# One Hymba-style layer: a two-part spread of 1 / rms, the mixer's first weights placed inside the FFN, and another order of the mixer's last norms

## The chip, the cores and the metric

The kernel runs on one core of one Trainium2 chip. The metric is the device time of one execution in microseconds. A core has a matrix engine (TensorE, PE in the profile; PEld is its loading of weights), a vector engine (VectorE, DVE), a scalar engine (ScalarE, ACT), GpSimd (POOL) and SyncE (SP), which here only issues transfers. Each engine takes its own instructions in the order in which the program lists them, and waits on semaphores where it needs the work of another.

## The reference, cut to what matters

1,048 tokens (16 meta tokens, 1,024 prompt tokens, 8 sample tokens) go through one decoder layer of width 1,024 in float32:

```
h = h + 0.5 * swiglu(rmsnorm(h, n1), w1g, w1u, w1d)      # first FFN, hidden width 2816
u = rmsnorm(h, nm) @ w_in                                # the mixer's input projection
...  HGRN2 scan of 4 heads (q, f, v, gate g); Mamba-2 scan of 8 heads (x, B, C after a short convolution, gate z, dt)
o_hg = o_hg * rsqrt(mean(o_hg^2) + eps) * hg_norm * silu(g)           # per head of 128
yz   = y * silu(z); yz = yz * rsqrt(mean(yz^2) + eps) * ssm_norm      # two groups of 256
h = h + concat(o_hg, yz) @ w_out
h = h + 0.5 * swiglu(rmsnorm(h, n2), w2g, w2u, w2d)      # second FFN
y = rmsnorm(h, norm_final)
```

The outputs are y and the new states of both scans and of the convolution.

## The kernel before, in words

Tokens lie along the free dimension of the tiles, features on the 128 partitions. The 1,048 tokens are four quarters of 262 (`Q`), two of which make a half. A float32 product with full accuracy is made of three products in the faster format float32r (`mm3`, lines 169 to 171): each operand is split into a rounded part `hi` and a rest `lo`, and hi·hi, hi·lo and lo·hi are summed in PSUM. A split is one cast on ScalarE (L163, L497, L376) and one subtraction on VectorE (L164, L501, L382).

**The first FFN** runs from 0 to about 699 us. Gate and up matrices and the down matrix are multiplied by a Strassen-like scheme of seven block products; the operands of half 0 are `ops[0]` (`o` in the code), those of half 1 `ops[1]` (`e`), and `cast`, `low` and `sum_` prepare block p of them. The work is a list of steps (class `Steps`): step i is a block of matrix products, 12 of them for a quarter and 4 input tiles, and `S.before(i, fn)` puts other work in front of step i. Inside `manual_schedule` the four engines PE, DVE, ACT and SP keep exactly this order of writing; instructions written after it are placed by the framework's planner, which may put them into gaps ahead.

The input tiles are normalised late: the FFN's first product uses x times the norm's weights, and 1 / rms of each token is multiplied into the results. `Input.rms` (before step 24) computes 1 / rms with tokens on partitions (`st[:, 1]`, ten columns for ten tiles of up to 128 tokens), then ScalarE scales a unit matrix by it, ten times (L1425): a diagonal matrix for every tile, side by side in one tile `diag` of 1,048 columns. `spread_r(q)` (before step 28 + q) multiplies a matrix of ones by a quarter of it in full float32 (L1430), which puts 1 / rms of each token on all partitions, and ScalarE copies that from PSUM (L1431) into the tile `spread`. The products `spread_r` have four PSUM buffers (`psm`) in common with other work, two of which the FFN's steps 26 to 31 hold.

The FFN's last 24 steps, before its end `e1`, are the seventh product of the down matrix: first half 0 for four pairs of output tiles, then, from `e0` = `e1` - 12, half 1 for the same. After each pair VectorE adds the result to h (L1118), ScalarE squares it (L255), VectorE adds the square (L256). From `e0` + 2 on, the mixer's norm of quarters 0 and 1 is made (L185 to L191), and from `e0` + 3 on, two jobs of `plain_x` before each step make the mixer's input x: for each of eight tiles of a quarter VectorE multiplies (L327), ScalarE casts (L328), VectorE subtracts (L330). 18 such jobs for quarters 0 and 1 stand before steps `e0` + 3 to `e0` + 11; those of quarters 2 and 3 stand at `e1`.

**The mixer** starts in `ssm_project`: `proj_first` multiplies the first chunk of 350 tokens with the weights of three units of 128 columns (units 0, 1, 2), then the second chunk, then the third. Each unit's weights are two raw tiles of 512 columns (`raw`, 8 buffers), split into two tiles `ws` (6 buffers) by L163 and L164. All this is written after the FFN, and the planner places it: it put the six splits ahead of and among the x jobs.

**The end of the mixer**: `Fill` hands out projections (`z1`, `g3` are the last) as filling between the scans. Then come the norm of the second Mamba group (`ssm_norm(K, 1, ...)`, a list of seven functions with `Rms.root`, `newton`, four `part`s) and that of HGRN head 3 (`hgrn_out(K, 3, ...)`). `root` sums squares by products of 32 columns (L209), ScalarE takes the root by Ln and Exp after loading a table (L211 to L217), VectorE refines it (L221 to L223), `part` spreads it again (L229). The first norm's functions all stand before the second norm's. Then `out_proj` multiplies with w_out.

Of the kernel before, what the change touches and what calls it, by code (L numbers as in the profile page):

```python
# [17 lines left out]
P = 128  # L18
# [49 lines left out]
class Core:  # L68
# [72 lines left out]

    def ws(self, dt=F32R):
        return self.wsp.tile([P, 1024], dt, tag="ws", name=self.uid("ws"))

    def weights(self, ap):

# [14 lines left out]
    def split(self, src, hi, lo):  # L161

        self.nc.scalar.copy(hi, src)  # L163
        self.nc.vector.tensor_sub(lo, src, hi.bitcast(F32))  # L164
# [150 lines left out]
def new_x(K):  # L315
    K.xhi, K.xlo = ([K.slot("u", T, F32R) for k in range(KT)] for i in range(2))
# [159 lines left out]
class Left:  # L476
# [732 lines left out]
def constants(K, a):  # L1209
    nc = K.nc  # L1210
    cst = K.const
    K.ident = cst.tile([P, P], F32, name="ident")
    make_identity(nc, K.ident)
    K.ones = {}
    for n in (1, D):
        K.ones[n] = cst.tile([P, P], F32, name=f"ones{n}")
        nc.vector.memset(K.ones[n], 1.0 / n)
    K.eps = cst.tile([P, 1], F32, name="eps")
# [88 lines left out]
class Input:  # L1307
# [111 lines left out]
    def rms(self):  # L1419

        K = self.K
        token_rstd(K, *(self.st[:, j] for j in range(3)))
        self.diag = K.slot("u", T)
        for i, (t0, n) in enumerate(self.tiles):
            K.nc.scalar.activation(self.diag[:, t0 : t0 + n], K.ident[:, :n], AF.Identity, scale=self.st[:, 1, i : i + 1])  # L1425

    def spread_r(self, q):
        K = self.K
        ps = K.psm()[:, :Q]
        K.nc.tensor.matmul(ps, K.ones[1], self.diag[:, q * Q : q * Q + Q], start=True, stop=True)  # L1430
        K.nc.scalar.copy(self.spread.quarter(q), ps)  # L1431


# [23 lines left out]
def ssm_project(K, a, o):  # L1457

    nc = K.nc
    wv = a["w_in"][0].rearrange("(k p) c -> p k c", p=P)  # L1460
    pc = K.pc


    rw = K.st0.tile([P, KT, 8])
    nc.sync.dma_start(rw, wv[:, :, C_DT : C_DT + 8])
    wd = K.sml.tile([P, KT, 16], F32R, tag="wdt", name="wdt", bufs=1)
    nc.scalar.copy(wd[:, :, 0:8], rw)
    nc.vector.tensor_sub(wd[:, :, 8:16], rw, wd[:, :, 0:8].bitcast(F32))
# [12 lines left out]
    nc.sync.dma_start(sc, a["state_conv"].rearrange("l b j c -> (l b j) c"))  # L1481
    ps = K.psm()
    for k in range(8):
        nc.tensor.transpose(ps[:, 24 * k : 24 * k + 24], sc[:, k * P : (k + 1) * P], K.ident[:24, :24])
    sb = K.st0.tile([P, 8, 8, 3])

    tails = K.st0.tile([P, 11, 8])
    nc.vector.tensor_copy(sb.rearrange("p k b j -> p (k b j)"), ps[:, :192])

    K.xs = []  # L1490

    def unit(k):
# [10 lines left out]
        return (*K.weights(wv[:, :, C_X + k * P : C_X + (k + 1) * P]), ev)  # L1503
# [721 lines left out]
def body(ctx, tc, a, o):  # L2225
# [10 lines left out]
    def before(S, i, *fns):  # L2236
        for fn in fns:
            S.before(i, (lambda fn=fn: fn[0](*fn[1:])))

    def first1(S, w, w2):  # L2240
# [73 lines left out]
        before(S, 27, (e.low, 5), (e.cast, 7))  # L2314
        before(S, 28, (e.low, 7))
        for q in range(4):
            before(S, 28 + q, (x.spread_r, q))
        before(S, 33, (e.cast, 4))
        before(S, 34, (e.low, 4))

    def after1(S, h, e3, e0, e1):
# [17 lines left out]
        for q in (1, 3):  # L2339
            S.before(e3 + q + 7, lambda q=q: nm.begin(q))  # L2340
            S.before(e3 + q + 9, lambda q=q: nm.finish(q))
        S.before(e0, lambda: new_x(K))
        S.before(e0 + 2, lambda: nm.end(0))
        S.before(e0 + 2, lambda: x_mix(0))
# [35 lines left out]
    with K.tc.manual_schedule(engines={mybir.EngineType.PE}):  # L2380
# [29 lines left out]
                kept.append(g)  # L2410
        fill.until("z1")
        fill(4)
        for fn in ssm_norm(K, 1, "s", lambda: None):
            fill(3)
            fn()
        fill.until("g3")
    for i in range(len(opa), 4):
        opa.append(split_spilled(i))
    for fn in hgrn_out(K, 3, pieces, us[3]["g"], "u", lambda: None):
        fn()  # L2420
    kept.append(us[3]["g"])
    kept += [y[:, NM:] for y in K.y[2:]]
    K.tokens(TO)
# [144 lines left out]
```

## Time and profile before

| | us |
|---|---|
| median of 3 runs | 1923.13 (1920.56 to 1923.39) |
| the profiled execution's own time | 1922.67 |
| its span, first to last instruction | 1920.9 |
| PE busy | 1905.5 (99%) |
| DVE busy | 1526.5 (79%) |
| ACT busy | 858.0 (45%) |

The granted clock of TensorE is 0.998 of full speed. The ends of products are modelled in such a profile, so the distance from one product's start to the next one's is read, not its length: in the FFN a float32r product of 262 columns starts 0.12 us after the one before it. In a row of the timeline stand the start, the length, the engine, the line, the operation, what it writes and reads, its shape and count, and in brackets the engine's idle time before it with what ended it.

### The profile page before, as it was taken

What the parts mean: (1) busy time and instruction counts of PE and PEld (TensorE: products, weight loads), DVE (VectorE), ACT (ScalarE), POOL (GpSimd) and SP (SyncE); (2) the same over time, 40 slices, a digit from 0 to 9 for tenths busy, and PEclk for the clock granted to TensorE, in tenths of its full rate; (3) what the DMA queues carried; (4) which work ended last, traced back from release to release, by engine and by line L of the source; (5) the groups of instructions that cost most, each with busy time, mean ns of one, the idle gap of its engine ahead of it and who ended that gap; (6) DMA issues with size and microseconds to landing.
All of it is one profiled execution on the core that took longest, in us unless ns stands there. A gap on an engine that the chain in (4) does not pass through costs nothing.

```text
span 1920.9 us, 41195 instructions
## 1 busy us (share of the span) xinstructions
PE 1905.5 (99%) x16692; PEld 1875.2 (98%) x16692; DVE 1526.5 (79%) x2866; ACT 858.0 (45%) x1635; POOL 30.1 (2%) x88
## 2 busy tenths in 40 slices
PE   9999999999999999999999999999999999999998
PEld 9999999999999999999999999999999999999998
DVE  7888888889788877566585557999888888978974
ACT  6533333334534644466564545743333332453353
POOL 3000000000000000000000000000000000000000
PEclk9999999999999999999999999999999999999999
DMA  7143333335967541221463254133333333596852
GB/s 249 50 128 95 95 107 112 92 98 175 305 215 243 165 152 52 66 89 38 116 186 85 83 173 144 58 114 107 99 93 101 101 112 93 173 269 210 281 175 84
DMA packets 324209, 258.46 MB, mean 135 GB/s; under 512 B 18923, under 2 KB 298731, under 8 KB 324011
## 3 DMA queue, kind: packets, MB, share of 16 engines
q1 hardware_dynamic: 323779, 255.79, 43.1%
q8 instruction: 131, 2.15, 0.5%
q14 instruction: 59, 0.48, 0.1%
q0 software_dynamic: 224, 0.04, 0.0%
q10 hardware_dynamic: 16, 0.00, 0.0%
HBM read 190.79 MB, written 65.05 MB: 133 GB/s over the span
## 4 chain that ended last, share of the span: by engine, by line
PE 94%; DVE 3%; ACT 1%; issue 1%; DMA 0%; SPq 0%; DVEq 0%; ACTq 0%
PE acc L169 24%; PE acc L171 23%; PE acc L170 23%; PE mis L169 5%; PE mis L170 5%; PE mis L171 5%; PE mis L1963 1%; DVE u L382 1%; DVE u L367 1%; PE mis L1665 0%; PE mis L2030 0%; PE mis L1659 0%; DMA s<-in_x_prompt_dram 0%; PE mis L2055 0%; PE mis L1654 0%
## 5 line engine op out<-in xcount | busy, mean ns | idle before, releaser
L169 PE MATMUL acc<-u,ws 128*128 128x258 f32 (+4 forms) x3634 | 1064.0, 293 | 1.1 <-DVE u L1279 0.8
L171 PE MATMUL acc<-u,ws 128*128 128x258 f32 (+4 forms) x3634 | 1055.3, 290 | 0.7 <-DVE ws L501 0.7
L170 PE MATMUL acc<-u,ws 128*128 128x258 f32 (+4 forms) x3634 | 1054.8, 290 | 0.0
L169 PEld LDWEIGHTS acc<-u,ws 128*128 128x128 f32 x3634 | 686.5, 189 | 8.7 <-issue 6.2
L170 PEld LDWEIGHTS acc<-u,ws 128*128 128x128 f32 x3634 | 688.3, 189 | 0.8 <-DVE u L330 0.2
L171 PEld LDWEIGHTS acc<-u,ws 128*128 128x128 f32 x3634 | 686.1, 189 | 1.6 <-DVE ws L501 1.1
L169 PE MATMUL mis<-u,ws 128*128 128x262 f32 (+1 forms) x810 | 230.2, 284 | 0.0
L171 PE MATMUL mis<-u,ws 128*128 128x262 f32 (+1 forms) x810 | 228.7, 282 | 0.0
L170 PE MATMUL mis<-u,ws 128*128 128x262 f32 (+1 forms) x738 | 208.6, 283 | 0.0
L501 DVE TENSOR_TENSOR ws<-r,ws 128x512 fp32r<-128x512 f32 x266 | 181.6, 684 | 4.1 <-ACT ws L497 3.9
L901 ACT ACTIVATE t<-t 128x524 f32<-128x524 f32 (+1 forms) x72 | 46.1, 640 | 300.1 <-DVE t L898 300.1
L497 ACT CAST ws<-r 128x512 fp32r<-128x512 f32 x266 | 156.8, 615 | 42.2 <-PE mis L171 18.1
L169 PEld LDWEIGHTS mis<-u,ws 128*128 128x128 f32 x810 | 152.9, 189 | 0.1
L171 PEld LDWEIGHTS mis<-u,ws 128*128 128x128 f32 x810 | 152.7, 189 | 0.0
L170 PEld LDWEIGHTS mis<-u,ws 128*128 128x128 f32 x738 | 139.9, 190 | 0.1
L493 DVE TENSOR_TENSOR r<-r,r 128x512 f32<-128x512 f32 x150 | 100.8, 684 | 0.3
L1031 DVE TENSOR_TENSOR u<-u,u 128x1048 fp32r<-128x1048 f32 (+3 forms) x84 | 96.1, 1146 | 4.8 <-ACT u L1027 4.3
L1089 ACT CAST ws<-u 128x512 fp32r<-128x512 f32 (+1 forms) x72 | 42.1, 585 | 109.9 <-DVE u L1084 105.2
L164 DVE TENSOR_TENSOR ws<-r,ws 128x512 fp32r<-128x512 f32 x88 | 59.5, 685 | 38.3 <-ACT ws L163 38.0
L1027 ACT CAST u<-u 128x1048 fp32r<-128x1048 f32 (+3 forms) x84 | 82.8, 988 | 1.3 <-DMA u<-hd 1.3
L1118 DVE SCALAR_TENSOR_TENSOR s<-acc,s 128x524 f32<-128x524 f32 (+3 forms) x86 | 53.9, 651 | 35.3 <-PE acc L171 35.0
L898 DVE TENSOR_TENSOR t<-t,u 128x524 f32<-128x524 f32 (+1 forms) x108 | 73.2, 692 | 0.1
(465 smaller groups left out, 2329.1 us busy)
## 6 DMA issues: line engine op xcount, KB each, us to landing
r<-in_w_ffn_down_dram SPq DMA_DIRECT2D x128, 256.0 KB
hd<-s SPq DMA_DIRECT2D x93, 258.0 KB
r<-in_w_ffn_gate_dram SPq DMA_DIRECT2D x88, 256.0 KB
r<-in_w_ffn_up_dram SPq DMA_DIRECT2D x88, 256.0 KB
hd<-s SPq DMA_DIRECT2D x77, 262.0 KB
u<-hd SPq DMA_DIRECT2D x36, 516.0 KB
u<-hd SPq DMA_DIRECT2D x28, 524.0 KB
r<-in_w_in_dram SPq DMA_DIRECT2D x56, 256.0 KB
```

Source lines behind the costliest of these rows:

```text
L164: self.nc.vector.tensor_sub(lo, src, hi.bitcast(F32))
L169: mm(ps, whi, xhi, start=first, stop=False, skip_group_check=more)
L170: mm(ps, whi, xlo, start=False, stop=False, skip_group_check=more)
L171: mm(ps, wlo, xhi, start=False, stop=last, skip_group_check=more)
L493: self.K.nc.vector.tensor_tensor(self.raw[p], self.raw[x], self.raw[y], op)
L497: self.K.nc.scalar.copy(self.w[p][:, : self.n * P], self.raw[p])
L501: self.K.nc.vector.tensor_sub(t[:, 512 : 512 + w], self.raw[p], t[:, :w].bitcast(F32))
L898: nc.vector.tensor_mul(t, t if src is None else src, spread.lanes(n, slice(0, 2)))
L901: nc.scalar.activation(t, t, AF.Silu)
L1027: K.nc.scalar.copy(hi, lo.bitcast(F32))
L1031: K.nc.vector.tensor_sub(lo, lo.bitcast(F32), hi.bitcast(F32))
L1118: nc.vector.scalar_tensor_tensor(t, b, 0.5, t, ALU.mult, ALU.add)
```

## The change

Three parts.

1. `Input.rms` no longer makes the diagonal matrices. It splits 1 / rms into a float32r part and the rest (`parts`, two small VectorE instructions). `diagonal(q)`, before step 26 + q, scales the unit matrix by both parts for quarter q, cut where tiles cross the quarter: six ScalarE instructions a quarter, 24 in all in place of ten, into a tile of the pool `t` (9 buffers) in place of one of the pool `u`. `spread_r(q)` sums two float32r products with a float32r matrix of ones, in place of one in float32.
2. The weights of the mixer's units 0 and 1 are loaded before steps `e1` - 11 and `e1` - 9 and split before steps `e1` - 4 and `e1` - 2, in the written order of the FFN. Unit 2's stay with the planner.
3. At the mixer's end the split of the last spilled operand moves ahead of both norms; the second norm's `root` follows the first norm's, and the rest of both norms' functions comes after that.

```diff
+        self.parts = K.sml.tile([P, 2, 10], F32R, tag="rp", name="rp", bufs=1)
+        K.nc.vector.tensor_copy(self.parts[:, 0], self.st[:, 1])
+        K.nc.vector.tensor_sub(self.parts[:, 1], self.st[:, 1], self.parts[:, 0].bitcast(F32))
...
+    def diagonal(self, q):
+        K = self.K
+        self.diag[q] = K.tmp.tile([P, 2 * Q], F32R, tag="t", name=K.uid("t"), bufs=9)
         for i, (t0, n) in enumerate(self.tiles):
-            K.nc.scalar.activation(self.diag[:, t0 : t0 + n], K.ident[:, :n], AF.Identity, scale=self.st[:, 1, i : i + 1])
+            c0, c1 = max(t0, q * Q), min(t0 + n, q * Q + Q)
+            for j in range(2):
+                if c0 < c1:
+                    K.nc.scalar.activation(self.diag[q][:, j * Q + c0 - q * Q : j * Q + c1 - q * Q], K.ident[:, c0 - t0 : c1 - t0], AF.Identity, scale=self.parts[:, j, i : i + 1].bitcast(F32))
...
-        K.nc.tensor.matmul(ps, K.ones[1], self.diag[:, q * Q : q * Q + Q], start=True, stop=True)
+        for j in range(2):
+            K.nc.tensor.matmul(ps, K.onesr, self.diag[q][:, j * Q : j * Q + Q], start=j == 0, stop=j == 1)
...
+            before(S, 26 + q, (x.diagonal, q))
             before(S, 28 + q, (x.spread_r, q))
...
+        for k, at, to in ((0, e1 - 11, e1 - 4), (1, e1 - 9, e1 - 2)):
+
+            def load(k=k):
+                raws[k] = K.weights_load(wv[:, :, C_X + k * P : C_X + (k + 1) * P])
+
+            def split(k=k):
+                K.pre[k] = K.weights_split(raws[k], P)
+
+            S.before(at, load)
+            S.before(to, split)
...
-        for fn in ssm_norm(K, 1, "s", lambda: None):
-            fill(3)
+        for i in range(len(opa), 4):
+            opa.append(split_spilled(i))
+        na = ssm_norm(K, 1, "s", lambda: None)
+        fill(3)
+        na[0]()
+        fill.until("g3")
+        nb = hgrn_out(K, 3, pieces, us[3]["g"], "u", lambda: None)
+        nb[0]()
+        for fn in (*na[1:], *nb[1:]):
             fn()
-        fill.until("g3")
-    for i in range(len(opa), 4):
-        opa.append(split_spilled(i))
-    for fn in hgrn_out(K, 3, pieces, us[3]["g"], "u", lambda: None):
-        fn()
```

More of the change, by code (lines that the diff above doesn't have):

```diff
@@ L143, in ws, with weights_load, weights_split @@
         return self.wsp.tile([P, 1024], dt, tag="ws", name=self.uid("ws"))
+    def weights_load(self, ap):
+        n, raws = 512 // ap.shape[-1], []
+        for k in range(0, ap.shape[1], n):
+            raws.append(self.raw())
+            self.nc.sync.dma_start(raws[-1].rearrange("p (k c) -> p k c", k=n), ap[:, k : k + n])
+        return raws
+    def weights_split(self, raws, c):
+        out = [self.split_w(raw) for raw in raws]
+        return [[t[:, 512 * i + k * c : 512 * i + k * c + c] for t in out for k in range(512 // c)] for i in range(2)]
     def weights(self, ap):
@@ L1217, in constants @@
         nc.vector.memset(K.ones[n], 1.0 / n)
+    K.onesr = cst.tile([P, P], F32R, name="onesr")
+    nc.vector.tensor_copy(K.onesr, K.ones[1])
     K.eps = cst.tile([P, 1], F32, name="eps")
@@ L1422, in rms @@
         token_rstd(K, *(self.st[:, j] for j in range(3)))
-        self.diag = K.slot("u", T)
+        self.parts = K.sml.tile([P, 2, 10], F32R, tag="rp", name="rp", bufs=1)
+        K.nc.vector.tensor_copy(self.parts[:, 0], self.st[:, 1])
+        K.nc.vector.tensor_sub(self.parts[:, 1], self.st[:, 1], self.parts[:, 0].bitcast(F32))
+        self.diag = {}
+    def diagonal(self, q):
+        K = self.K
+        self.diag[q] = K.tmp.tile([P, 2 * Q], F32R, tag="t", name=K.uid("t"), bufs=9)
         for i, (t0, n) in enumerate(self.tiles):
-            K.nc.scalar.activation(self.diag[:, t0 : t0 + n], K.ident[:, :n], AF.Identity, scale=self.st[:, 1, i : i + 1])
+            c0, c1 = max(t0, q * Q), min(t0 + n, q * Q + Q)
+            for j in range(2):
+                if c0 < c1:
+                    K.nc.scalar.activation(self.diag[q][:, j * Q + c0 - q * Q : j * Q + c1 - q * Q], K.ident[:, c0 - t0 : c1 - t0], AF.Identity, scale=self.parts[:, j, i : i + 1].bitcast(F32))
     def spread_r(self, q):
@@ L1501, in ev @@
                 conv(k, rt)
-        return (*K.weights(wv[:, :, C_X + k * P : C_X + (k + 1) * P]), ev)
+        return (*(K.pre.pop(k) if k in K.pre else K.weights(wv[:, :, C_X + k * P : C_X + (k + 1) * P])), ev)
     def conv(k, rt):
@@ L2341, in after1 @@
             S.before(e3 + q + 9, lambda q=q: nm.finish(q))
+        wv = a["w_in"][0].rearrange("(k p) c -> p k c", p=P)
+        raws, K.pre = {}, {}
+        for k, at, to in ((0, e1 - 11, e1 - 4), (1, e1 - 9, e1 - 2)):
[5 more added lines that the diff above has]
+            S.before(to, split)
         S.before(e0, lambda: new_x(K))
```

## The prediction

> **What bounds the kernel now.** I read the page's busy times first, then the waits of TensorE, then the timeline at the three places that the change touches.
>
> ```profile
> span 1920.9 us, 41195 instructions
> PE 1905.5 (99%) x16692; PEld 1875.2 (98%) x16692; DVE 1526.5 (79%) x2866; ACT 858.0 (45%) x1635; POOL 30.1 (2%) x88
> ```
>
> TensorE is the bound everywhere: time can only be won by shorter products or where it stands still. The waits of TensorE say how little that is:
>
> ```profile
> PE mis L1343 <- DMA s<-in_x_prompt_dram: 2.1, 2, 1.9
> ...
> PE acc L169 <- DVE u L1279: 0.8, 1, 0.8
> PE acc L171 <- DVE ws L501: 0.7, 2, 0.4
> ...
> PE mis L1430 <- ACT u L1431: 0.5, 1, 0.5
> PE mis L209 <- ACT s L1806: 0.4, 1, 0.4
> PE mis L1430 <- ACT u L1425: 0.4, 1, 0.4
> ```
>
> Columns: who waited for whom, us in total, times, longest. The change aims at four of these rows (L1430 twice, L169, L209): 2.1 us together, 0.11% of the time. So the sum is small whatever happens, and a new wait of one or two us turns its sign. What releases TensorE at these places are ScalarE and VectorE, so each part is worked out on their queues.
>
> **Part 1, the spread of 1 / rms (57 to 70 us).** TensorE, with the step between two usual products in the last pair of rows:
>
> ```profile
> 59.77 0.28 PE L171 MATMUL mis<-u,ws 128*128 128x262 f32 x1
> 60.45 0.71 PE L1430 MATMUL mis<-u,ones 128*128 128x262 f32 x2 [0.40 <-ACT u L1425]
> ...
> 62.46 0.60 PE L1430 MATMUL mis<-u,ones 128*128 128x262 f32 x2
> ...
> 63.02 0.29 PE L170 MATMUL acc<-u,ws 128*128 128x262 f32 x1
> ...
> 68.80 0.28 PE L171 MATMUL mis<-u,ws 128*128 128x262 f32 x1
> 68.92 0.28 PE L169 MATMUL acc<-u,ws 128*128 128x262 f32 x1
> ```
>
> A usual product takes 68.92 - 68.80 = 0.12 us. From 62.46 to 63.02 lie one spread and one usual product: 0.56 - 0.12 = 0.44 us for the float32 spread. Two float32r products in its place: 0.24. That removes 4 x 0.20 = 0.8 us of work. [...]
>
> ScalarE and VectorE decide when the spreads can start:
>
> ```profile
> L1425 ACT ACTIVATE u<-ident,st x10: 288/387/403, 59.4 to 62.0; 128x128 f32<-128x128 f32 x8, 128x12 f32<-128x12 f32 x2
> ```
>
> ```profile
> 58.04 0.21 ACT L1442 ACTIVATE st<-st 128x10 f32<-128x10 f32 x1 [2.42 <-DVE st L1441]
> 59.41 2.84 ACT L1425 ACTIVATE u<-ident,st 128x128 f32<-128x128 f32 x10 [1.16 <-DVE st L1451]
> 62.16 2.02 ACT L376 CAST u<-u 128x1048 fp32r<-128x1048 f32 x2
> 64.58 0.38 ACT L1431 COPY u<-mis 128x262 f32<-128x262 f32 x1 [0.41 <-PE acc L171]
> ```
>
> ```profile
> 59.15 0.17 DVE L1451 TENSOR_TENSOR st<-st 128x10 f32<-128x10 f32 x1
> ...
> 63.24 2.41 DVE L382 TENSOR_TENSOR u<-u,u 128x1048 fp32r<-128x1048 f32 x2 [3.31 <-ACT u L376]
> ```
>
> Ten diagonal instructions take 62.16 - 59.41 = 2.75 us; the two short ones are 0.1 us shorter, so a long one costs 0.295 and a short one 0.195. A quarter now needs two parts of three pieces, one of them short: 4 x 0.295 + 2 x 0.195 = 1.57 us, 6.3 for all, 3.5 more than before. The written order on ScalarE becomes: cast of e's block 5, diagonal 0, cast of 7, diagonal 1, diagonal 2, copy 0, diagonal 3, copy 1. The first cast fits into the 1.16 idle us before 59.41, and VectorE's subtraction for it into its 3.31. That is a gain for those engines, not for TensorE. The rest, step by step:
> - Two more VectorE instructions of about 0.2 us behind L1451; diagonal 0 starts at 59.6 with the first part and is whole at 61.3. TensorE, free at 59.89, starts the spread at 61.35 instead of 60.45. Then 0.24 and a step of 12 x 0.122 = 1.46: 63.05.
> - The other cast (1.0) and diagonal 1: ScalarE is through at 63.8. TensorE waits 0.85, and its step ends at 65.6.
> - Diagonal 2 is ready at 65.4, but spread 2 needs the PSUM buffer that copy 0 frees, at 65.7. Its step ends at 67.45.
> - Diagonal 3 ends at 67.5, copy 1 at 67.8; spread 3 at 67.87, its step ends at 69.57. Before, the next step began at 68.92.
>
> So part 1 costs 0.65 us: two shorter waits have become four, because ScalarE, not the float32 product, sets the pace. The bounds: if no wait is left, 0.8 and the two waits of 0.9 are won, -1.7. At worst the weight cast that follows copy 1 on ScalarE, and VectorE's work behind it, passes its whole delay of some 2.3 us on. I take +0.7, since the chain above is made of the rows nearest to it. The float32r ones matrix and the smaller claim on pool `u` cost nothing: the first 12 us wait for x by the 2.1 us row.
>
> **Part 2, the mixer's first weights (683 to 713 us).** VectorE, then ScalarE, then TensorE:
>
> ```profile
> 685.42 1.35 DVE L164 TENSOR_TENSOR ws<-r,ws 128x512 fp32r<-128x512 f32 x2 [1.50 <-ACT ws L163]
> ...
> 687.48 0.43 DVE L190 SCALAR_TENSOR_TENSOR t<-mis,t 128x262 f32<-128x262 f32 x1
> 687.82 0.68 DVE L164 TENSOR_TENSOR ws<-r,ws 128x512 fp32r<-128x512 f32 x1
> 688.42 0.42 DVE L191 SCALAR_TENSOR_TENSOR t<-t,t 128x262 f32<-128x262 f32 x1
> ...
> 698.75 0.89 DVE L327 SCALAR_TENSOR_TENSOR t<-s,col,t 128x262 f32<-128x262 f32 x2
> ...
> 699.72 0.43 DVE L330 TENSOR_TENSOR u<-t,u 128x262 fp32r<-128x262 f32 x1
> ...
> 706.46 0.42 DVE L1118 SCALAR_TENSOR_TENSOR s<-acc,s 128x262 f32<-128x262 f32 x1
> ...
> 711.83 0.90 DVE L327 SCALAR_TENSOR_TENSOR t<-s,col,t 128x262 f32<-128x262 f32 x2
> ```
>
> ```profile
> 684.77 1.28 ACT L163 CAST ws<-r 128x512 fp32r<-128x512 f32 x2
> ...
> 699.27 0.81 ACT L328 CAST u<-t 128x262 fp32r<-128x262 f32 x2 [0.90 <-DVE t L327]
> ```
>
> ```profile
> 698.67 0.28 PE L171 MATMUL acc<-u,u 128*128 128x262 f32 x1
> 699.74 0.59 PE L169 MATMUL acc<-u,ws 128*128 128x350 f32 x2 [0.78 <-DVE u L1279]
> ...
> 700.48 0.32 PE L171 MATMUL acc<-u,ws 128*128 128x350 f32 x1
> ...
> 712.83 0.58 PE L169 MATMUL acc<-u,ws 128*128 128x350 f32 x2
> ```
>
> ```profile
> 684.00:700.60 16.60, 15.82 (x126) 15.38 (x125) 14.22 (x35) 10.23 (x22) 0.30 (x3) 1.00 0.66 195
> ```
>
> In this last row, of the busy times by stretch, the columns after the length are PE, PEld, DVE and ACT: VectorE is idle 2.4 us, of which 1.5 lie before 685.42. TensorE ends the FFN at 698.8 and is in full swing at 700.48: 1.5 us lost, because VectorE makes the first tile of quarter 1 only then (L327 at 698.75, L330 at 699.72; they are jobs 9 and 10 of the 18). In these queues VectorE lies up to 8 us behind TensorE: its last L1118 of the FFN runs at 706.46. The planner's first two splits (685.42) lie in VectorE's idle time and cost nothing; of the next two, one delays L191 by 688.42 - 687.95 = 0.47, the other hides a wait. Taken out of there, units 0 and 1 give back some 0.45 us. Put before `e1` - 4, the split of unit 0 stands behind job 9 and ahead of job 10: job 9's L327 ends at 698.8 instead of 699.2, its cast at 699.2, two weight casts take 1.28 (first ready at 699.8), and VectorE, next in whose queue is the first subtraction, stands 1.05 us, then works 1.2: job 10 starts at 701.05, and L330 of the first tile ends at 701.9 in place of 700.15. The split of unit 1, behind four more jobs, does the same again: its weights are there at 706.1 to 707.4, and the last L1118 moves from 706.46 to about 710.0. Behind it queue the norm and x of quarters 2 and 3, which chunk 2 needs: 711.83 - 706.46 = 5.4 us, now 715.4, a cast later 715.9.
>
> Nothing of that is hidden: TensorE has only units 0 and 2 to work on and waits 698.8 to 701.9 but for a product or two, and again for tiles 2 and 4. Chunk 1 of the three units takes 712.83 - 700.48 = 12.35 us from its fourth product. With unit 1 last it would end near 715.3, 2.5 later than before; the small projection for dt could fill idle time, which brings it down to +1.0. I take +2.6, the start of chunk 2 that both queues give. Below, the best case is that the 1.5 us go entirely: -1.5. Above is the first rival. The transfers cost nothing: eight raw buffers are free that early either way.
>
> **Part 3, the mixer's end.**
>
> ```profile
> 1151.87 0.72 PE L229 MATMUL mis<-t,ones 1*128 1x258 f32 x8
> 1153.00 0.64 PE L209 MATMUL mis<-u,ones 128*32 128x258 f32 x8 [0.42 <-ACT s L1806]
> 1153.57 0.39 PE L169 MATMUL acc<-u,ws 128*128 128x258 f32 x1
> ```
>
> The second norm's sums (L209, 1153.00) wait for copies of the first norm's spread, while products of `out_proj` stand behind them. Moved up beside the first norm's L209, they wait for nothing that is late, and the 0.42 goes, with some 0.2 for one entry into small products less: -0.6. Lower bound -1.0 (all but the eight's own 0.72 between 1151.87 and 1153.57). If the second norm's spread is put too early behind the first's it could wait for ScalarE's and VectorE's second chain: +2. The early split of the last operand is ahead of its use anyway.
>
> **Sum.** 1922.67 (the profiled execution's own time) + 0.7 + 2.6 - 0.6 = 1925.4; the median of the runs lies 0.46 above that execution, so 1925.8. A measurement of this kernel can tell about 0.2%, 3.85 us, from no change: between 1919.3 and 1927.0 it is the same. Its own range, by the nearer bounds: 1922.5 to 1927.
>
> **Rivals.** *Slower: TensorE meets unit 1 early.* Its order is fixed before the run. If unit 1's products stand interleaved with those of units 0 and 2, TensorE stops at the first of them until 706.1, with six products done; what is left of the 12.35 us, 11.9, then ends at 718.0, 5.2 later than 712.83. Sum: 0.7 + 5.2 - 0.6 = +5.3, 1928.4. It decides as soon as fewer than some twelve products stand ahead of it. For it: three units were interleaved before, the first two rows being two L169 in a row. Against: the planner places products by when it expects weights. That TensorE does not pass a waiting product is what the row at 1153.00 shows. [...]
>
> *Faster: all aimed-at waits go.* Then -1.7 - 1.5 - 1.0 = -4.2, 1918.9. It needs ScalarE's diagonals and VectorE's splits to lie in idle time. Against it: VectorE has hardly any after 685.42 (the row by stretch), and ScalarE has 3.5 us more to do in a stretch of 9.
>
> *No difference by another way:* the waits move by less than I say, and 1923 stays.
>
> **Chances.** Within 0.2%: 0.50 (forecast 0.38, the last rival 0.12). Slower 0.35, nearly all the first rival. Faster 0.15. The range from 1918.5 to 1930 leaves out about 0.1 at each end.
>
> **What would show it.** Part 1: L1430 pairs of 0.24, each with a bracket for L1425's successor or the copy; the first product after step 31 near 69.6. Part 2: L164 twice in VectorE's row between the 9th and 10th L327, TensorE's first full product group after 701.5, chunk 2 after 715. Part 3: two L209 groups side by side and no bracket at the second. I am wrong if VectorE reaches job 9 well before 698, if the planner's later work lets unit 0's split run early, or if the other mixer stages, which the planner places anew, gain or lose waits of their own.

## The result

The changed kernel is slower. Six runs have a median of 1929.47 us (1927.27 to 1932.08), beside them six runs of the kernel before 1922.94 us. The difference of the medians is 6.5 us, and the ratio is 1.0038 with a 95% interval of 1.0025 to 1.0051. I had forecast 1925.8 us, which was +2.7 on the median then known and lay inside the 0.2% that I called no difference.

The profiled execution took 1929.86 us, 7.2 us more than the one of before. The head of its page, then its waits of TensorE (who waited for whom, us in total, times, longest):

```profile
span 1928.1 us, 41207 instructions
PE 1909.5 (99%) x16692; PEld 1879.4 (97%) x16692; DVE 1526.7 (79%) x2869; ACT 861.4 (45%) x1649; POOL 30.5 (2%) x88
```

```profile
PE acc L183 <- DVE u L343: 3.0, 2, 1.6
...
PE mis L1456 <- ACT t L1450: 1.5, 2, 1.0
...
PE mis L242 <- DVE t L236: 1.3, 1, 1.3
```

Each part has brought a wait of its own. Line numbers are 13 to 26 higher than before: L183 is a product of three (L170 before), L343 the last step of an x tile (L330), L1456 the spread (L1430), L1450 its diagonal (L1425), L242 the product of a gate (L229).

To see where the time goes I follow each product of TensorE through both traces and take how much later it starts. That lag grows in steps:

| stretch of the kernel before, us | growth of the lag, us | what lies there |
|---|---|---|
| 0 to 57 | +0.9 | the start, where x is waited for |
| 57 to 70 | +0.5 | the spreads of part 1 |
| 70 to 690 | +1.3 | products only, nothing of the change |
| 690 to 745 | +5.2 | the splits of part 2 |
| 745 to 760 | -1.5 | a stretch at half clock, which of these two profiles only that of before has |
| 760 to 1205 | +0.2 | among it part 3 |
| 1205 to 1900 | +0.7 | products only |

The spreads on TensorE in the changed kernel (start, us, name, in brackets the idle time ahead):

```profile
61.98 0.57 PE L1456 MATMUL mis<-t,onesr 128*128 128x262 f32 x2 [1.01 <-ACT t L1450]
62.40 0.28 PE L182 MATMUL acc<-u,ws 128*128 128x262 f32 x1
...
64.49 0.58 PE L1456 MATMUL mis<-t,onesr 128*128 128x262 f32 x2 [0.48 <-ACT t L1450]
...
66.37 0.53 PE L1456 MATMUL mis<-t,onesr 128*128 128x262 f32 x2
66.74 0.28 PE L182 MATMUL mis<-u,ws 128*128 128x262 f32 x1
...
68.42 0.58 PE L1456 MATMUL mis<-t,onesr 128*128 128x262 f32 x2
```

ScalarE makes the diagonals in 1.65 us a quarter, and the first two spreads wait for it. From the start of a pair of spread products to the next product lie 0.37 to 0.42 us (66.37 to 66.74, 61.98 to 62.40), where the prediction had 0.24.

At the mixer's start, VectorE and then TensorE:

```profile
699.87 0.48 DVE L340 SCALAR_TENSOR_TENSOR t<-s,col,t 128x262 f32<-128x262 f32 x1
...
701.35 1.29 DVE L177 TENSOR_TENSOR ws<-r,ws 128x512 fp32r<-128x512 f32 x2 [0.66 <-ACT ws L176]
...
707.60 1.29 DVE L177 TENSOR_TENSOR ws<-r,ws 128x512 fp32r<-128x512 f32 x2 [0.57 <-ACT ws L176]
...
711.99 0.42 DVE L1131 SCALAR_TENSOR_TENSOR s<-acc,s 128x262 f32<-128x262 f32 x1
```

```profile
701.46 0.34 PE L182 MATMUL acc<-u,ws 128*128 128x350 f32 x1
703.45 0.43 PE L183 MATMUL acc<-u,ws 128*128 128x350 f32 x1 [1.65 <-DVE u L343]
...
706.26 0.66 PE L183 MATMUL acc<-u,ws 128*128 128x350 f32 x1 [1.32 <-DVE u L343]
706.72 0.50 PE L184 MATMUL acc<-u,ws 128*128 128x350 f32 x1
707.01 0.49 PE L182 MATMUL acc<-u,ws 128*128 128x350 f32 x1
```

The splits (L177) stand in VectorE's queue where the prediction put them, and TensorE waits twice behind them. The last two rows hold what I had not foreseen: behind the second wait the products start 0.29 us apart instead of 0.16. The busy times by stretch show why (length, PE busy, then the granted clock):

```profile
698.63:702.05 3.42, 3.17 (x26) 1.00 0.53 110
702.05:705.46 3.41, 1.49 (x6) 1.00 0.59 166
705.46:708.87 3.41, 2.61 (x9) 0.50 0.39 145
708.87:712.29 3.42, 3.42 (x14) 0.50 0.56 153
```

After 3.41 us in which TensorE was busy for 1.49, the clock is halved for twice 3.41 us. Of the 5.3 us that the lag grows between 690 and 721 us, the two waits are 3.0.

### The profile page after: what moved, and what is told of

The parts are those of the page before. It is cut to its first block, busy times and chain, and to the rows that moved or that the text cites. A ratio compares the mean times of both kernels' runs of the same rounds, so it can differ in the third digit from the quotient of the medians.

```text
span 1928.1 us, 41207 instructions
## 1 busy us (share of the span) xinstructions
PE 1909.5 (99%) x16692; PEld 1879.4 (97%) x16692; DVE 1526.7 (79%) x2869; ACT 861.4 (45%) x1649; POOL 30.5 (2%) x88
## 4 chain that ended last, share of the span: by engine, by line
PE 93%; DVE 4%; ACT 2%; issue 1%; DMA 0%; DVEq 0%; SPq 0%; ACTq 0%
PE acc L182 24%; PE acc L184 23%; PE acc L183 23%; PE mis L184 5%; PE mis L182 5%; PE mis L183 5%; PE mis L1989 1%; DVE u L395 1%; DVE u L380 1%; PE mis L1691 0%; PE mis L2056 0%; PE mis L1685 0%; PE mis L2081 0%; PE mis L1680 0%; PE mis L1978 0%
## 5 line engine op out<-in xcount | busy, mean ns | idle before, releaser
L183 PE MATMUL acc<-u,ws 128*128 128x258 f32 (+4 forms) x3634 | 1055.3, 291 | 3.0 <-DVE u L343 3.0
L183 PEld LDWEIGHTS acc<-u,ws 128*128 128x128 f32 x3634 | 688.1, 189 | 4.9 <-DVE u L343 3.9
L183 PE MATMUL mis<-u,ws 128*128 128x262 f32 (+1 forms) x738 | 208.5, 283 | 0.0
L183 PEld LDWEIGHTS mis<-u,ws 128*128 128x128 f32 x738 | 139.8, 189 | 0.0
L177 DVE TENSOR_TENSOR ws<-r,ws 128x512 fp32r<-128x512 f32 x88 | 59.4, 685 | 39.3 <-ACT ws L176 38.9
```

Source lines behind the costliest of these rows:

```text
L183: mm(ps, whi, xlo, start=False, stop=False, skip_group_check=more)
```

## The experiments

Each kernel is timed beside the kernel before on the same chip; ratios carry 95% intervals.

**Each part alone, and the change without part 2.** The edits are the parts of the diff shown above, applied to the kernel before:

```diff
 only_spread (with rms(), diagonal() and spread_r() of the change)
+    K.onesr = cst.tile([P, P], F32R, name="onesr")
...
+            before(S, 26 + q, (x.diagonal, q))

 only_weights (with weights_load() and weights_split() of the change)
+        for k, at, to in ((0, e1 - 11, e1 - 4), (1, e1 - 9, e1 - 2)):
...
+            S.before(at, load)
+            S.before(to, split)

 only_order
...
+        nb = hgrn_out(K, 3, pieces, us[3]["g"], "u", lambda: None)
+        nb[0]()
+        for fn in (*na[1:], *nb[1:]):
             fn()

 no_weights: only_spread and only_order together
```

> Part 1 alone (two-part spread, the constant onesr at the start, diagonals on ScalarE). Theory A, read from the two traces (most of the slowdown is part 2, where idle time of TensorE around the splits also takes its clock down): part 1 costs the +0.5 us seen between 57 and 70 us plus the +0.1 to +0.85 us seen in the first 15 us, so 0.5 to 1.4 us above the kernel before. Rival B (the slowdown is spread evenly over the three parts, part 1 a third of +6.5): +2 us or more. My forecast for the part was +0.7.

> Part 2 alone (the mixer's first weights loaded and split inside the FFN). Theory A: the kernel is 3.5 to 5.5 us slower than before; the waits of L183 for u of L343 (1.65 and 1.32 us in the changed kernel) are there, and TensorE's granted clock is 0.5 for one or two stretches of 3.41 us right behind them. Rival B (a third): +2 us. My forecast for the part was +2.6, without any change of the clock: if the waits are there and the clock stays full, the time is near +2.6.

> Part 3 alone (the order of the mixer's last norms). Theory A, from the offsets in the two traces (-1.0 us where the roots come together, +1.35 us where L242 waits for t of L236): +0.0 to +0.5 us. My forecast for the part: -0.6 (bounds -1.0 to +2). Rival B (a third of the slowdown): +2 us.

> Parts 1 and 3 without part 2. Theory A: 0.5 to 1.9 us above the kernel before, that is 4 to 6 us under the changed kernel, and no stretch at half clock near 705 us. Rival B: +4 us. If the three parts simply add, this run is the sum of the runs with part 1 alone and part 3 alone.

| kernel | median, us | before, us | ratio (interval) |
|---|---|---|---|
| part 1 alone | 1924.92 | 1921.96 | 1.0016 (1.0007 to 1.0025) |
| part 2 alone | 1926.51 | 1921.96 | 1.0023 (1.0013 to 1.0032) |
| part 3 alone | 1922.72 | 1921.96 | 1.0006 (0.9998 to 1.0015) |
| parts 1 and 3 | 1926.77 | 1921.96 | 1.0026 (1.0015 to 1.0037) |

Part 2 is the largest, +4.5 us, as theory A had it, and part 3 is within the uncertainty. But part 1 costs +3.0 us, not 0.5 to 1.4, and parts 1 and 3 together +4.8 (the two alone make 3.8): here the first theory falls. Followed product by product, part 1 alone loses 0.5 us between 57 and 70 us; +1.25 us come evenly between 120 and 690 us, and +0.8 between 1205 and 1900 us, where nothing of part 1 runs. The row of busy times for one and the same 560 us shows it, PE's busy time and its products right behind the length; kernel before first, then part 1 alone:

```profile
130.00:690.00 560.00, 560.00 (x4600) 559.81 (x4599) 470.58 (x803) 220.35 (x388) 0.16 (x1) 1.00 0.50 155
```

```profile
130.00:690.00 560.00, 560.00 (x4589) 559.81 (x4589) 468.96 (x800) 220.13 (x386) 0.17 (x1) 1.00 0.50 154
```

TensorE is busy all the time in both, at full clock (1.00), and gets through 11 products less; at 0.122 us each these are 1.3 us. The kernels with parts 1 and 3 and with all parts show the same slope, as I call this slow growth of the lag (4590 products in both); those with part 2 or part 3 alone do not (4599 and 4600).

In the profile of part 2 alone the two waits are there as in the changed kernel, but the clock stayed full:

```profile
700.49 0.43 PE L183 MATMUL acc<-u,ws 128*128 128x350 f32 x1 [1.65 <-DVE u L343]
...
703.30 0.43 PE L183 MATMUL acc<-u,ws 128*128 128x350 f32 x1 [1.32 <-DVE u L343]
703.58 0.32 PE L184 MATMUL acc<-u,ws 128*128 128x350 f32 x1
703.74 0.32 PE L182 MATMUL acc<-u,ws 128*128 128x350 f32 x1
```

Between 690 and 721 us the lag grows by 3.4 us here and by 5.3 in the changed kernel, so the half clock is worth 1.9 us. In the profiles of the kernel before and of the change, every later change of the clock lies a whole number of times 3.413 us behind the first full clock (217, 218 and 559 times; 204, 206 and 561 times). Laid out so here, the stretch of 3.41 us with the second wait holds more products than the one that went before the half clock in the changed kernel (x9, of which eight start in it, and 2.09 us busy; there x6 and 1.49 us):

```profile
700.57:703.98 3.41, 2.09 (x9) 1.00 0.91 304
```

Whether that is why the clock stayed full, no run shows. This profiled execution (1924.32 us) was the quickest of ten; the others took 1.4 to 3.4 us more, and there is no trace to show whether they lost it to half clock.

**Where part 1's slope comes from.** `onesr` takes 512 bytes in the first pool and `rp` another 80, so every later tile starts 512 or, with rounding, 608 bytes further on.

```diff
 pad
+    K.pads = cst.tile([P, P], F32, name="pad"), K.sml.tile([P, 2, 10], F32, tag="pad", name="pad", bufs=1)

 spread_inplace (against part 1 alone)
-    for n in (1, D):
-        K.ones[n] = cst.tile([P, P], F32, name=f"ones{n}")
-        nc.vector.memset(K.ones[n], 1.0 / n)
-    K.onesr = cst.tile([P, P], F32R, name="onesr")
-    nc.vector.tensor_copy(K.onesr, K.ones[1])
+    K.onesr = cst.tile([P, P], F32R, name="ones1")
+    K.ones[D] = cst.tile([P, P], F32, name=f"ones{D}")
+    nc.vector.memset(K.ones[D], 1.0 / D)
+    nc.vector.tensor_scalar(K.onesr, K.ones[D], float(D), None, ALU.mult)
+    K.ones[1] = K.onesr[:, :].bitcast(F32)
...
-        self.parts = K.sml.tile([P, 2, 10], F32R, tag="rp", name="rp", bufs=1)
+        self.parts = K.sml.tile([P, KT, 16], F32R, tag="wdt", name="rp", bufs=1)[:, 0:2, 0:10]
```

> The kernel before with two tiles that nothing reads or writes (512 bytes in the pool of constants, 80 in the pool of small tiles), so that every tile behind them lies 512 to 608 bytes further on, as in the kernels with part 1; no instruction is added. In the run with part 1 alone, 2.1 of its +3.0 us come in steps of under 1 ns per product, between 120 and 700 us (+1.2) and 1300 and 1900 us (+0.9), far from anything that part 1 does. Theory A (the places of the tiles in SBUF cause this): about +2 us against the kernel before, with the same two slopes. Rival B (the extra products, or the order in which buffers are taken, cause it): no difference, and no slope.

> Part 1 without new room: the float32r ones take the place of the float32 ones (read as float32 where float32 is wanted), and the two parts of 1 / rms lie in a small tile that the mixer uses later; the buffers of x, weights and products start where they started before. Theory A (places in SBUF): what is left is what is seen at its place, +0.5 to +1.0 us, and no slope. Rival B (extra products, or the turn of the buffers, which this kernel has too): +3 us as with part 1 alone, with the slopes.

With the pad alone: 1924.02 us beside 1922.31, ratio 1.0008 (0.9999 to 1.0016). With the spread in old room: 1922.44 beside 1922.31, ratio 1.0000 (0.9991 to 1.0009). The same 560 us, pad first, then the spread in old room:

```profile
130.00:690.00 560.00, 560.00 (x4596) 559.81 (x4595) 469.93 (x802) 220.38 (x387) 0.17 (x1) 1.00 0.51 155
```

```profile
130.00:690.00 560.00, 560.00 (x4600) 559.81 (x4599) 470.06 (x802) 220.69 (x387) 0.16 (x1) 1.00 0.51 155
```

Two tiles that no instruction touches slow the products of a long stretch by one in a thousand, and part 1 without new room is free of the slope there, though it has the same products and takes its other buffers in the same turn. The count of products is steady enough to tell: it is 4599 to 4601 in the twelve profiles without new room, 4589 or 4590 in the four with part 1's new room, and 4596 with the pad. The whole time with the pad (+1.7 us) is just not clear of no difference.

The pad doesn't give the whole slope. Between 130 and 690 us the lag grows by 0.5 us with the pad, by 1.2 with part 1 and by 0.05 with the spread in old room; between 1205 and 1890 us by 0.65, by 0.8 and by -0.65. So new room and the other turn of the buffers (the diagonals are in tiles `t`, no longer in one of `u`) act together, and the spread in old room even gains in the second stretch, which is why its time is under what theory A gave. Room is a cause; which tiles must lie how was not found. (Between 892 and 1135 us the pad loses 2.3 us, some 1.5 of it in a stretch of 3.41 us at half clock from 892.66 us.)

**Where part 2's splits may stand.** In the kernel before, the planner has all six splits of the three units done early; in the change they begin 16 us later, 13 in the run with part 2 alone. One row per kernel, before and change (durations, then first and last start):

```profile
L164 DVE TENSOR_TENSOR ws<-r,ws x6: 681/684/694, 685.4 to 692.2; 128x512 fp32r<-128x512 f32 x6
```

```profile
L177 DVE TENSOR_TENSOR ws<-r,ws x6: 683/686/692, 701.4 to 712.3; 128x512 fp32r<-128x512 f32 x6
```

```diff
 (all against part 2 alone)
 weights_early
-        for k, at, to in ((0, e1 - 11, e1 - 4), (1, e1 - 9, e1 - 2)):
+        for k, at, to in ((0, e1 - 11, e1 - 9), (1, e1 - 9, e1 - 7)):
 weights_first
+        for k, at, to in ((0, e1 - 11, e1 - 10), (1, e1 - 9, e1 - 8)):
 loads_only
-            S.before(to, split)
...
-        return (*(K.pre.pop(k) if k in K.pre else ...
+        return (*(K.weights_split(K.pre.pop(k), P) if k in K.pre else ...
 weights_filled (busy: 14 products)
+                K.nc.tensor.matmul(ps, K.xhi[0][:, :P], K.xhi[0][:, : 2 * P], start=True, stop=True)
...
+        S.before(e1, busy)
```

> Part 2 alone, the same loads, but the splits five steps of the last down-projection earlier (in front of the mixer's first input products instead of between the last of them). Theory A (the splits' place in VectorE's written order holds up the x that unit 0 needs, and the idle time now and then takes the clock down): the waits of L183 for u of L343 (3.0 us in sum with part 2 alone) fall under 1.5 us, time 0 to +1.5 us against the kernel before, 3 to 4.5 us under part 2 alone. Rival B (unit 0 comes too early for its x whatever is split when: the order of TensorE is the cause): the waits stay near 3 us, time +3.5 to +5.

> Part 2 alone with 14 products that nothing reads (256 columns, about 0.11 us each, 1.5 us in all) on TensorE behind the last step of the FFN, where it otherwise stands for about 1.6 us. Theory A1 (part 2's price is 3.3 us of waits and the rest, some 1.2 us in the median, is half clock that follows the gap in part of the runs): the median falls by 0.5 to 1.5 us against part 2 alone, to +3 to +4, and no stretch at half clock lies between 700 and 715 us. Rival A2 (the waits alone are the price): no change or a loss of up to 0.5 us, because unit 0's own first products start behind the fill.

> Half of part 2: units 0 and 1 are loaded inside the FFN as in part 2, but they are split where the mixer takes them, so that the planner places the splits, as it did before. With part 2 the first of these subtractions runs at 698.4 us, where the kernel before had all six of units 0 to 2 done by 692.9 us, the first two in idle time of VectorE (685.42). Theory A (the written place of the splits is the cause, not the loads and not TensorE's order): the splits are back between 685 and 693 us, and the time is that of the kernel before, -0.5 to +1 us. Rival B (the loads on SP, or the earlier units in TensorE's order): +3 to +5, as with the whole of part 2.

> Part 2 with the splits six steps earlier than in the change, that is one step before the run with early splits: the first stands ahead of the norm's chain of quarter 0 (nm.end(0)) instead of behind it. With early splits, unit 0 was split at 689.9 us, behind that chain, the planner put unit 2's splits behind unit 1's (695.3 to 698.3), and TensorE stood 3.9 us. Theory A (VectorE's work between 685 and 699 us is what is short, and the idle 1.5 us before 685.42 must be used): the first split falls into that idle time, the stand of TensorE shrinks by about 1.4 us against the early splits, and the time is +2.5 to +4 us against the kernel before. Rival B (each written place costs the same): +5 as with the early splits. Rival C (ahead of the chain there is no cost): 0 to +1.

| kernel | median, us | before, us | ratio (interval) | splits on VectorE, first to last start |
|---|---|---|---|---|
| part 2 alone | 1926.51 | 1921.96 | 1.0023 (1.0013 to 1.0032) | 698.4 to 709.4 |
| weights_early | 1927.25 | 1922.31 | 1.0025 (1.0015 to 1.0036) | 689.9 to 697.6 |
| weights_first | 1927.05 | 1921.62 | 1.0031 (1.0019 to 1.0042) | 683.4 to 694.6 |
| loads_only | 1921.89 | 1921.62 | 1.0001 (0.9992 to 1.0010) | 686.3 to 693.1 |
| weights_filled | 1928.15 | 1922.31 | 1.0034 (1.0021 to 1.0046) | 698.6 to 709.6 |

With the loads alone moved, the planner puts the splits back, and the whole cost of part 2 is gone, so the loads cost nothing. But with the splits TensorE's order goes back too. In the runs with part 2 as it is, the planner gives TensorE another order at the mixer's start: one hi·hi product, then products that need the rest of the first x tile, where the kernel before has two hi·hi products side by side. Between 700 and 721 us, 66 places hold another of the three kinds of product than before. With loads_only, weights_early and weights_first every place holds the kind and shape that it holds in the kernel before. The last two still cost 4.9 and 5.4 us, so the written place of the splits costs without another order; what the order adds in part 2 itself no run separates.

No written place that I tried does better: early splits exchange two waits of 1.65 and 1.32 us for one longer wait, here with the splits that come first:

```profile
701.38 0.59 PE L182 MATMUL acc<-u,ws 128*128 128x350 f32 x2 [3.64 <-DVE u L1292]
```

(The row names L1292, a small operation of VectorE that ends at 701.35; ScalarE's cast of an x tile ends at 701.33, and the trace doesn't tell which of the two counted.) The busy times fit a reason, VectorE's being the third figure with a count; the kernel before, then the run with the splits first, its stretch set 1.2 us earlier because it runs ahead by that:

```profile
680.00:690.00 10.00, 10.00 (x83) 9.94 (x82) 5.17 (x11) 5.60 (x10) 0.16 (x1) 1.00 0.50 160
```

```profile
678.80:688.80 10.00, 10.00 (x83) 9.94 (x82) 3.77 (x8) 3.94 (x6) 0.16 (x1) 1.00 0.50 160
```

Two of the six splits fall into the idle time of these 10 us in the run with the splits first, but the planner had fitted in four, between the links of the norm's chain. The 1.4 us that VectorE does less here are two splits of 0.69, and they are done later, in a stretch in which it has no time to spare. With early splits it is 3.23 us instead of 5.17, and the wait 3.75. Of my three theories for the run with the splits first, B met the time (+5.4 us). A's sum was wrong: one of the two pairs came early, and the wait shrank by 0.1 us, not by 1.4. That VectorE's time here is what is short remains argued from the busy times.

The fill missed its aim. The 14 products of `busy` (256 columns, into a PSUM tile that nothing reads) stand behind the FFN in TensorE's order, yet the mixer's first products were placed ahead of them:

```profile
700.73 0.43 PE L183 MATMUL acc<-u,ws 128*128 128x350 f32 x1 [1.65 <-DVE u L343]
703.54 0.66 PE L183 MATMUL acc<-u,ws 128*128 128x350 f32 x1 [1.32 <-DVE u L343]
...
711.73 2.03 PE L2345 MATMUL mis<-u 128*128 128x256 f32 x14
```

They filled no wait, and the kernel is 5.8 us slower than before, where part 2 alone was 4.5. Whether a fill would have kept the clock stays open.

**Parts 1 and 3 done otherwise.**

```diff
 order_later (against part 3 alone)
-        for fn in (*na[1:], *nb[1:]):
+        for fn in na[1:]:
             fn()
+    for fn in nb[1:]:
         fn()

 spread_balanced (against spread_inplace; all four diagonals at step 25)
+                    if j:
+                        K.nc.vector.tensor_scalar(d, s, w, None, ALU.mult)
+                    else:
+                        K.nc.scalar.activation(d, s, AF.Identity, scale=w)
...
-        before(S, 27, (e.low, 5), (e.cast, 7))
-        before(S, 28, (e.low, 7))
+        before(S, 27, (e.low, 5))
+        before(S, 28, (e.cast, 7))
+        before(S, 29, (e.low, 7))
```

> Part 3 alone, but only the second norm's sums stand beside the first's; its Newton steps and gates are again left to the planner, as in the kernel before, so that products of the output projection can stand ahead of its spreads. Theory A (part 3 wins 1.0 us with the sums together and loses 1.35 us because the gates' products wait in written order for VectorE's Newton steps): that wait goes, -0.5 to -1.0 us against the kernel before, about 1.5 us under part 3 alone. Rival B (the wait only moves): +0.0 to +0.8.

> Part 1 in the old room, with the low parts of the diagonals on VectorE, all diagonals ahead of the casts of blocks 5 and 7, and the cast of block 7 behind the first spread. Theory A (in part 1 ScalarE's twelve long diagonals set the pace of the spreads, at 0.3 us each): the waits ahead of L1456 fall from 1.5 to about 0.5 us, and between 57 and 70 us the kernel gains 0.8 to 1.7 us on the kernel before instead of losing 0.5. Rival B (what is spared in front of the spreads comes back at the blocks whose cast is later): no gain between 57 and 75 us. In the whole time either is within the uncertainty, so the stretch decides.

With the gates later: 1923.16 us beside 1921.62, ratio 1.0010 (1.0001 to 1.0019). The remaining steps of the second norm now stand behind the order that is written for TensorE. The first norm's spreads and the second's gates, with that edit and then with part 3 alone:

```profile
1152.02 0.72 PE L229 MATMUL mis<-t,ones 1*128 1x258 f32 x8
1154.09 0.72 PE L229 MATMUL mis<-t,ones 1*128 1x258 f32 x8 [1.35 <-ACT s L1806]
```

```profile
1152.93 0.72 PE L229 MATMUL mis<-t,ones 1*128 1x258 f32 x8
1154.99 0.72 PE L229 MATMUL mis<-t,ones 1*128 1x258 f32 x8 [1.35 <-ACT s L1806]
```

The edit changed nothing: TensorE and ScalarE have the same instructions in the same order in both kernels, the planner leaves the gates where they were written, and both kernels lose 0.44 us between 1135 and 1205 us. So theory A was not tested, and the time (+1.5 us) lies above both ranges; in its profile a lag of 1.9 us stands before 57 us already, with a half clock from 12.85 us. Nor does the trace say what the gates wait for: with part 3 alone ScalarE's fourth copy of the first norm's spread ends at 1154.86 us and VectorE's last Newton step at 1154.85, and in the changed kernel the row names the Newton step.

With the work of the spreads shared: 1920.57 us beside 1921.62, ratio 0.9996 (0.9987 to 1.0005). One wait of 0.49 is left:

```profile
60.37 0.51 PE L1447 MATMUL mis<-t,ones 128*128 128x262 f32 x2 [0.49 <-ACT t L1441]
...
62.18 0.41 PE L1447 MATMUL mis<-t,ones 128*128 128x262 f32 x2
62.42 0.28 PE L169 MATMUL acc<-u,ws 128*128 128x262 f32 x1
...
63.93 0.51 PE L1447 MATMUL mis<-t,ones 128*128 128x262 f32 x2
...
65.75 0.41 PE L1447 MATMUL mis<-t,ones 128*128 128x262 f32 x2
```

Between 57 and 70 us this kernel gains 1.3 us on the kernel before, 0.15 of it is given back by 80 us. That is what theory A gave: ScalarE's diagonals had set the pace. Two of the four pairs now take the 0.24 us of the prediction (62.18 to 62.42). In the whole time this is the best of the kernels, but not told apart from the kernel before.

**One cause out, the other, both.**

```diff
 after_inplace   the change, with part 1 as in spread_inplace
 after_planned   the change, with part 2 as in loads_only
 mended          the change, with both
```

> The changed kernel, with part 1 in old room (as in the run with the spread in place), parts 2 and 3 as they are. Theory A (two causes, which add: tiles moved in SBUF 2 to 3 us, splits in a written place 4 to 5 us): +4 to +5.5 us against the kernel before, 2 to 3 us under the change. Rival B (moved tiles are a small cost of part 1 alone, and the change's loss is part 2's): +6 to +7.

> The changed kernel with its early loads, but with the splits of units 0 and 1 left to the planner; parts 1 and 3 as they are. Theory A: the splits are again done by about 694 us, and what is left is parts 1 and 3: +3 to +5 us (part 1 and 3 together measured +4.8, the two alone +3.0 and +0.8). Rival B (the planner, with part 1's other buffers, puts them elsewhere, or TensorE's order costs it): +6 to +7.

> The changed kernel with both causes out: part 1 in old room, splits left to the planner; part 3 as it is. Theory A: only part 3's +0.8 and the +0.0 to +0.5 of the spreads' waits are left, +0.3 to +1.3 us against the kernel before, within 0.2% of it, 5 to 6 us under the change. Rival B (a third cause that shows only with the parts together): +2 us or more.

| kernel | median, us | before, us | ratio (interval) |
|---|---|---|---|
| after_inplace | 1928.60 | 1921.53 | 1.0034 (1.0021 to 1.0047) |
| after_planned | 1927.14 | 1921.53 | 1.0028 (1.0017 to 1.0038) |
| mended | 1923.11 | 1921.53 | 1.0006 (0.9997 to 1.0015) |

With both causes out the change is within the uncertainty of the kernel before (+1.6 us, theory A 0.3 to 1.3), and no third cause is needed, though the interval leaves room for a small one. The other two runs missed what theory A gave. Without new room the kernel is 7.1 us slower, no better than the change (+6.5), as rival B had it; with the planner's splits it is 5.6 us slower, between A's +3 to +5 and B's +6 to +7. So the times don't confirm that the two costs add, and with intervals of 4 to 5 us they can't refute it either.

The traces show the slope's part: without new room, 4599 products stand in the 560 us instead of 4590, and the lag grows by 0.1 us between 70 and 690 us instead of 1.3. In that kernel the splits again cost 5.3 us with twice 3.41 us of half clock. With the planner's splits this stretch costs nothing, but its profile has stretches of 3.41 us at half clock elsewhere, from 12.56, 896.61 and 1159.44 us, of which the last two cost 1.5 us each. Apart from the first microseconds and the end, the seventeen profiles (the two kernels and fifteen runs) have such stretches at five places (12.6 to 16.6, 702 to 712, 747 to 756, 892 to 900, 1158 to 1163 us), some at three of them, part 2 alone at none. What moves a time is thus partly which of them it meets.

## Why the prediction was wrong

The sign of the whole and the order of the parts were right, the size was off: +2.7 forecast, +6.5 measured. By its steps:

- *Part 1 at its place, "+0.65 us"*: near, partly by luck. The lag grows by 0.45 to 0.5 us, and ScalarE sets the pace as worked out. But the pair of products took 0.37 to 0.42 us, not 0.24, so against 0.44 it saved 0.02 to 0.07 each time and not 0.20; and TensorE stood three times, 2.0 us in all from start to start, where the chain has four stands of 2.8. The two errors nearly cancel.
- *"The float32r ones matrix and the smaller claim on pool `u` cost nothing"*: this step failed. I asked only when the matrix is made, not where it lies. It moves all tiles behind it, and with part 1 alone the products between 120 and 690 and after 1205 us are slower by about 1 in 450 and 1 in 900; in the changed kernel's trace that is 1.3 + 0.7 = 2.0 us. Part 1 alone cost 3.0 us, and 0.1 with its tiles in old room.
- *Part 2, "+2.6"*: the mechanism was right. The splits stood where I put them, the waits were two (3.0 us; at full clock the stretch loses 3.4), and leaving the splits to the planner removes them. The term was mis-sized: at full clock it was 0.8 us too small, and I priced the stand of TensorE at its own length, while 6.83 us at half clock followed, 1.9 us more.
- *The clock*, of which no step of the prediction spoke: in the changed kernel two waits of 1.65 and 1.32 us and a stretch of 3.41 us with 1.49 us of work stand ahead of 6.83 us at half clock. With part 2 alone the same two waits, with 2.09 us of work in the stretch of the second, left it at full (1.00).
- *Part 2's best case, "-1.5"*, needed the splits to use VectorE's idle time. The planner already did so; four of its six splits were in that time or between the norm's steps.
- *Part 3, "-0.6"*: wrong, +0.44 in the trace of part 3 alone (its time, +0.8, is within the uncertainty). The wait of 0.42 before the second sums did go. In its place came the one whose price I bounded at +2, the second spread behind the first, 1.35 us.
- *The rival "TensorE meets unit 1 early"* gave 1928.4, near the measured time, but it isn't what happened: behind the second wait, which was for x, TensorE ran on (with part 2 alone it stood once more, for 0.3 us), and with the loads moved and the planner's splits the time is that of before.
- *The sum*: 0.7 + 2.6 - 0.6 stands against 3.0 + 4.5 + 0.8 for the parts alone, which is more than the 6.5 of all three; whether they add is open. The 0.9 us in the first row of the table are hardly the change: in kernels with the same first 57 us as before this lag lies anywhere from -1.2 (weights_first, at full clock from 5.63 us) to +1.9 (order_later, at half clock from 12.85 to 16.27 us); the changed kernel came to full clock at 9.14 us, the kernel before at 6.72.

## What to carry to other kernels

Before work that a planner places is written into a fixed order, look in the trace where it stands now: here the splits "moved forward" came 13 us later. Two stands of TensorE, of 1.65 and 1.32 us, cost 1.9 us more where 6.83 us at half clock followed them, and nothing more where the clock stayed full, so price both cases. And a new constant tile can have a price of its own in a kernel that is 99% products (part 1 alone cost 3.0 us, and 0.1 with its tiles in old room): try it where an old one lay.

## What was not expected of the hardware

- Products of the same form at full clock ran at 4600 or at 4589 in 560 us, depending on where tiles lie in SBUF. Two tiles of 512 and 80 bytes that are never touched were enough for 4596. On average a product comes later by 0.1 to 0.3 ns, and no wait shows it. It is no noise: with the loads alone moved, the 4597 products that start in this stretch keep their distances to the kernel before within 1 ns.
- The clock was lost without idle time, too. In the kernel before, the stretch ahead of its half clock is fully busy:

```profile
744.00:747.41 3.41, 3.41 (x28) 3.12 (x28) 1.90 (x6) 2.46 (x3) 0.00 (x0) 1.00 0.52 140
747.41:750.82 3.41, 3.41 (x12) 3.41 (x13) 3.29 (x13) 0.27 (x1) 0.00 (x0) 0.50 0.60 162
```

  Of the products that start in this stretch, 18 are small ones with 16 rows and 8 columns (L1540 and L1541), and eight have 350 columns. For the kernel before and the change I laid stretches of 3.41 us end to end from the first full clock, 547 and 546 at full clock between 25 and 1900 us, and counted every product with its columns, times its rows over 128. The median is 7336 in both. In each of the two the lowest count stands ahead of the half clock, 2818 in the stretch above and 2100 (six products of 350) in the change, and no other of these stretches has half clock behind it; the next lowest are 2984 and 3586. With part 2 alone the stretch with the second wait has eight products of 350, 2800, and the clock stayed full. So in these two traces the count tells the stretch that the busy share (3.41 of 3.41 us) doesn't, but the 2800 show that it isn't all; no run changed it alone, and a cause is not shown.
